# Cross-entropy with label smoothing: wider transfers in the first row, eleven shrinking ones in the second, buffers at multiples of 256 bytes, exponential sums in PSUM

## The chip, the cores and the metric

The kernel runs on one core of one Trainium2 chip. The metric is device time in microseconds of one execution; lower is better. The kernel before takes 84.87 us, the median of ten runs (84.70 to 84.98).

A core has several engines that run side by side, each through its own list of instructions: TensorE (matmul, PE in the profile), VectorE (DVE), ScalarE (ACT), GpSimd (POOL) and SyncE (SP), which here only issues DMA transfers. They wait for each other, and for transfers, on semaphores.

## The reference

The input is 256 rows of 32,000 logits in fp32, 256 labels and a smoothing of 0.1. For every row the loss is the negative sum of the smoothed targets times the log-probabilities:

```python
batch, num_classes = logits.shape                       # 256, 32000
log_probs = logits - np.max(logits, axis=-1, keepdims=True)
log_probs = log_probs - np.log(np.sum(np.exp(log_probs), axis=-1, keepdims=True))
smooth_targets = np.full((batch, num_classes), smoothing / num_classes)
for i, label in enumerate(labels):
    smooth_targets[i, label] = 1.0 - smoothing + smoothing / num_classes
return (-np.sum(smooth_targets * log_probs, axis=-1)).astype(np.float32)
```

The targets of a row sum to one, so the loss of a row is the logarithm of its sum of exponentials, minus `smoothing / num_classes` times the sum of its logits, minus `1 - smoothing` times the logit at its label. The kernel computes these three things. It does not subtract the maximum.

## The kernel before

The 256 rows are put on 128 partitions, two rows in each: partition p holds rows 2p and 2p + 1, one after the other, 64,000 columns in all. The kernel goes through the columns from left to right, first row first, in pieces whose widths stand in `WIDTHS` (lines 17 to 20): four of 8000 for the first row, and ten for the second, from 8000 down to 832.

For each piece there are three steps.

- `load` (line 156) issues one DMA transfer from SP's queue, 128 rows of one piece each. The very first piece goes in two halves, one from SP's queue and one from ScalarE's; a hook (`_issue_first_transfers_at_start`, line 40) moves these two issues to the start of the program. Pieces of 4736 columns or more rotate through three buffers of 8000 columns (`ring`); a piece that finds its buffer still in use makes SP wait until both VectorE and ScalarE are done with the old content, and all later issues stand behind it. Each smaller piece has a buffer of its own (`tail`).
- `sum_logits` (line 170) lets VectorE add the left half of the piece to the right half, with an accumulator that sums the result over the columns. The elementwise result goes to a scratch place (`jd`) and is not used.
- `sum_exps` (line 183) lets ScalarE compute the exponentials of the piece, again with an accumulator. The elementwise result, bf16, is not used either: for pieces over `TURN_MAX` = 3648 columns it goes to the one scratch place `ja`, for smaller ones to three places `jt` in turn.

An operation with an accumulator is two instructions in the profile: the main one, and a short READ_ACCUMULATOR that writes the 128 sums to their destination.

Around this, GpSimd loads the labels, gathers the logits at the labels and scales them (lines 104 to 152), and makes the identity matrix that TensorE needs for transposes.

The sums of the first row lie side by side in `sums0` (SBUF). When its four pieces are done, GpSimd adds them in two steps (`half`), ScalarE takes the logarithm (line 216), GpSimd puts the loss together (lines 218 to 224), TensorE turns the column of 128 losses into a row (`row_of`, line 190), and VectorE copies it to `res` (line 226).

The sums of the second row are finished in three layers, so that little is left after the last piece: the logit sums of the first eight pieces lie in `xsum` and the exponential sums of the first seven in `esum`, and are reduced to `done[0]` (lines 255 and 258) after VectorE's part of the third piece from the end. The last but two and the last but one exponential sums, and the last two logit sums, come through two small pairs (`pair0`, `pair1`), which are added to it (line 263). The exponential sum of the last piece goes to `elast` in PSUM and is the input of the last logarithm, with the sum of all the others as its bias (line 279). TensorE transposes both results, VectorE combines them to `res` (line 284), and SP stores the 256 losses.

Five pieces before the last, twenty matmul passes without use (`warm`, line 270) keep TensorE busy on the piece just loaded.

The order of the instructions on each engine is that of the program text, except where `tc.issue_after` names an instruction after which the next ones are to stand. The framework assigns the buffers and puts the semaphore waits in front of the instructions that need them.

Of the kernel before, what the change touches and what calls it, by code (L numbers as in the profile page):

```python
# [8 lines left out]
FP32 = mybir.dt.float32  # L9
BF16 = mybir.dt.bfloat16  # L10
I32 = mybir.dt.int32
ALU = mybir.AluOpType
AF = mybir.ActivationFunctionType
# [1 line left out]


WIDTHS = (
    (8000, 8000, 8000, 8000),
    (8000, 6272, 4736, 3648, 2688, 2048, 1536, 1216, 1024, 832),
)  # L20

RING_MIN = 4736

TURN_MAX = 3648

WARM_LEFT, WARM_COLS = 5, 256


def _exp_ln_table(arch: str) -> int | None:
# [30 lines left out]
def kernel(  # L60
# [7 lines left out]
    nc = tc.nc  # L68
    nc.at_finalize(_issue_first_transfers_at_start)
    B, C = logits.shape  # L70
    P = nc.NUM_PARTITIONS
    R = B // P
# [4 lines left out]
    c_small = eps / float(C)  # L77
    c_big = 1.0 - eps

    ring = ctx.enter_context(tc.tile_pool(name="ring", bufs=3))  # L80
    tail = ctx.enter_context(tc.tile_pool(name="tail", bufs=1))
    junk = ctx.enter_context(tc.tile_pool(name="junk", bufs=1))
    turn = ctx.enter_context(tc.tile_pool(name="turn", bufs=3))
    small = ctx.enter_context(tc.tile_pool(name="small", bufs=1))

    psum = ctx.enter_context(
        tc.tile_pool(name="psum", bufs=1, space=bass.MemoryType.PSUM)
    )

    tbl = _exp_ln_table(nc.m.arch)  # L90
    if tbl is not None:
        nc.scalar.add_instruction(  # L92
            mybir.InstLoadActFuncSet(
                name=nc.get_next_instruction_name(),
# [7 lines left out]
    x = logits.rearrange("(p r) c -> p (r c)", r=R)  # L102
# [3 lines left out]
        out=lab[:], in_=labels.bitcast(I32).rearrange("(p f) -> p f", p=P)  # L106
    )
    rowoff = small.tile([P, R], I32, name="rowoff", tag="rowoff")
    for r in range(R):
        nc.gpsimd.iota(  # L110
            out=rowoff[:, r : r + 1],
# [6 lines left out]
        out=flat_idx[:],  # L118
        in0=rowoff[:],
        in1=lab[:].rearrange("p (r two) -> p r two", two=2)[:, :, 0:1],  # L120
        op=ALU.add,
    )
    gat = small.tile([P, R], FP32, name="gat", tag="gat")
    for r in range(R):
        nc.gpsimd.indirect_dma_start(  # L125
            out=gat[:, r : r + 1],
            out_offset=None,
            in_=logits[:],
# [8 lines left out]

    label_weight = c_big / c_small
    xsum = small.tile([P, len(WIDTHS[-1]) + 1], FP32, name="xsum", tag="xsum")
    esum = small.tile([P, len(WIDTHS[-1])], FP32, name="esum", tag="esum")  # L140
    weighted = [
        small.tile([P, 1], FP32, name=f"weighted{r}", tag=f"weighted{r}")[:]
        for r in range(R - 1)
# [1 line left out]
    for r in range(R):  # L145
        nc.gpsimd.tensor_scalar(  # L146
            out=weighted[r],
            in0=gat[:, r : r + 1],
# [4 lines left out]

    res = small.tile([1, P, R], FP32, name="res", tag="res")

    def load(w: int, col: int, name: str):
        if w >= RING_MIN:
            xt = ring.tile([P, max(WIDTHS[0])], FP32, name="xt", tag="xt")
        else:
            xt = tail.tile([P, w], FP32, name=name, tag=name)  # L160
        if col == 0:

            h = w // 2
            nc.sync.dma_start(out=xt[:, :h], in_=x[:, :h])
            nc.scalar.dma_start(out=xt[:, h:w], in_=x[:, h:w])
        else:
            nc.sync.dma_start(out=xt[:, :w], in_=x[:, col : col + w])  # L167
        return xt

    def sum_logits(xt, w: int, out: bass.AP):  # L170
        h = w // 2
        jd = junk.tile([P, max(WIDTHS[0]) // 2], FP32, name="jd", tag="jd")
        return nc.vector.scalar_tensor_tensor(  # L173
            out=jd[:, :h],
            in0=xt[:, :h],
            scalar=1.0,
            in1=xt[:, h:w],
            op0=ALU.mult,
            op1=ALU.add,
            accum_out=out,  # L180
        )

    def sum_exps(xt, w: int, out: bass.AP) -> None:
        if w > TURN_MAX:
            ja = junk.tile([P, max(WIDTHS[0])], BF16, name="ja", tag="ja")
        else:
            ja = turn.tile([P, TURN_MAX], BF16, name="jt", tag="jt")
        nc.scalar.activation(out=ja[:, :w], in_=xt[:, :w], func=AF.Exp, accum_out=out)  # L188

    def row_of(column: bass.AP, name: str):  # L190

        row = psum.tile([1, P], FP32, name=name, tag=name)
        nc.tensor.transpose(out=row[:], in_=column, identity=ident[:])  # L193
        return row

    col = 0
    for r in range(R - 1):
        n = len(WIDTHS[r])
        sums = small.tile([P, 2, n], FP32, name=f"sums{r}", tag=f"sums{r}")
        for t, w in enumerate(WIDTHS[r]):  # L200
            xt = load(w, col, f"xl{r}_{t}")
            col += w
            sum_logits(xt, w, sums[:, 0, t : t + 1])
            sum_exps(xt, w, sums[:, 1, t : t + 1])


        while n > 1:
            assert n % 2 == 0
            n //= 2
            half = small.tile([P, 2, n], FP32, name=f"half{r}_{n}", tag=f"half{r}_{n}")  # L210
            nc.gpsimd.tensor_tensor(  # L211
                out=half[:], in0=sums[:, :, :n], in1=sums[:, :, n:], op=ALU.add
            )
            sums = half
        lse = small.tile([P, 1], FP32, name=f"lse{r}", tag=f"lse{r}")
        nc.scalar.activation(out=lse[:], in_=sums[:, 1, :], func=AF.Ln)  # L216
        lin = small.tile([P, 1], FP32, name=f"lin{r}", tag=f"lin{r}")
        nc.gpsimd.tensor_tensor(out=lin[:], in0=sums[:, 0, :], in1=weighted[r], op=ALU.add)
        scaled = small.tile([P, 1], FP32, name=f"scaled{r}", tag=f"scaled{r}")
        nc.gpsimd.tensor_scalar(  # L220
            out=scaled[:], in0=lin[:], scalar1=-c_small, scalar2=None, op0=ALU.mult
        )
        loss = small.tile([P, 1], FP32, name=f"loss{r}", tag=f"loss{r}")
        nc.gpsimd.tensor_tensor(out=loss[:], in0=scaled[:], in1=lse[:], op=ALU.add)  # L224
        loss_t = row_of(loss[:], f"loss_t{r}")
        nc.vector.tensor_copy(out=res[:, :, r : r + 1], in_=loss_t[:])  # L226

    r = R - 1  # L230
    n = len(WIDTHS[r])
    elast = psum.tile([P, 1], FP32, name="elast", tag="elast")
    pairs = [
        small.tile([P, 2], FP32, name=f"pair{i}", tag=f"pair{i}") for i in range(2)
    ]
    done = [
        small.tile([P, 2], FP32, name=f"done{i}", tag=f"done{i}") for i in range(3)
    ]
    warm = psum.tile([P, WARM_COLS], FP32, name="warm", tag="warm")
    for t, w in enumerate(WIDTHS[r]):  # L240
        left = n - 1 - t
        xt = load(w, col, f"xl{r}_{t}")
        col += w
        part = sum_logits(
            xt, w, xsum[:, t + 1 : t + 2] if left > 1 else pairs[1 - left][:, 0:1]
        )
        if left == 0:
            sum_exps(xt, w, elast[:])
        elif left <= 2:
            sum_exps(xt, w, pairs[2 - left][:, 1:2])  # L250
        else:
            sum_exps(xt, w, esum[:, t : t + 1])
        if left == 2:
            with tc.issue_after(part.ins):
                nc.vector.tensor_reduce(
                    out=done[0][:, 0:1], in_=xsum[:, : t + 2], axis=AX.X, op=ALU.add
                )
                nc.vector.tensor_reduce(
                    out=done[0][:, 1:2], in_=esum[:, :t], axis=AX.X, op=ALU.add
                )  # L260
        elif left < 2:
            i = 1 - left
            nc.vector.tensor_tensor(  # L263
                out=done[i + 1][:], in0=done[i][:], in1=pairs[i][:], op=ALU.add
            )
        if left == WARM_LEFT:


            for i in range(w // WARM_COLS):
                nc.tensor.matmul(  # L270
                    warm[:],
                    lhsT=ident[:],
                    rhs=xt[:, i * WARM_COLS : (i + 1) * WARM_COLS],
                    start=True,
                    stop=True,
                )

    lse = small.tile([P, 1], FP32, name=f"lse{r}", tag=f"lse{r}")
# [6 lines left out]
        out=res[:, :, r : r + 1],  # L285
        in0=lin_row[:],
        scalar=-c_small,
        in1=lse_t[:],
# [4 lines left out]
        out=out.rearrange("(g i) -> g i", g=1), in_=res[:].rearrange("g p r -> g (p r)")  # L293
# [36 lines left out]
```

## Time and profile before

| | us |
|---|---|
| median of ten runs | 84.87 |
| the profiled execution, in all | 84.89 |
| its span, from the first to the last instruction of the profile | 83.1 |
| ScalarE busy | 58.8 |
| VectorE busy | 37.1 |
| TensorE matmul busy | 7.3 |
| GpSimd busy | 5.9 |
| bytes moved by DMA | 32.77 MB, 394 GB/s over the span |
| start of the last exponential (832 columns) | 79.18 |
| start of the last logarithm | 80.15 |
| start of the last VectorE instruction (`res`) | 80.77 |

The profile is of one execution. Its own time is 84.89, 1.8 more than its span; the difference lies before the first and after the last instruction that the profile shows. All times below are counted from the start of the span.

The chain of waits, followed back from the end, goes through DMA for 64% of the span and through ScalarE for 32%. ScalarE sits idle for 19.9 us before its exponentials of pieces in the ring, and VectorE for 33.5 us before its sums of them, each time until a transfer lands. From 67.66 on, ScalarE works without a break that the chain shows: the seven exponentials of the smaller pieces, then the logarithm.

Of the instruction shapes that matter here, one exponential of 8000 columns takes 6.870 us, of 6272 columns 5.430, of 832 columns 0.879; one VectorE sum of 8000 columns 4.325, of 832 columns 0.592; an accumulator read on ScalarE 0.186 into SBUF and 0.149 into PSUM, on VectorE 0.082.

### The profile page before, as it was taken

Reading aid. Unit: us, or ns where it says so; the run is one execution under the profiler, and the core shown is the slowest. Engines: PE = TensorE matmul, PEld = TensorE weight load, DVE = VectorE, ACT = ScalarE, POOL = GpSimd, SP = SyncE. Lnnn points to the kernel's source line nnn. Section 1 sums busy time; section 2 is a strip of 40 time slices with the busy share of each in tenths; the row PEclk is TensorE's granted clock in tenths of the full one; section 3 lists DMA queues with packets and bytes.
Section 4 is the critical chain, followed back from the end, with each engine's and each line's share of the span. In section 5 each row is a group of like instructions: output and inputs, shape, how many; then the busy total and the mean of one; then the engine's idle time right before and its main releaser. Section 6 shows DMA issues by size and latency. Waiting matters only on the chain.

```text
span 83.1 us, 230 instructions
## 1 busy us (share of the span) xinstructions
PE 7.3 (9%) x23; PEld 5.3 (6%) x23; DVE 37.1 (45%) x35; ACT 58.8 (71%) x31; POOL 5.9 (7%) x19
## 2 busy tenths in 40 slices
PE   0000000000000000000000010000000000899220
PEld 0000000000000000000000000000000000778000
DVE  0000005950595009910397018922944735754860
ACT  5000005997599809994399908997999999999960
POOL 3201630041000000000000040000000000000000
PEclk9999999999999999999999999999999999999996
DMA  5999999998999899979997998998999999999600
GB/s 123 408 448 408 454 424 447 493 401 354 478 493 416 354 462 493 431 339 462 493 431 339 462 440 386 447 495 343 438 417 428 435 411 410 416 410 411 274 0 0
DMA packets 2258, 32.77 MB, mean 394 GB/s; under 512 B 337, under 2 KB 338, under 8 KB 850
## 3 DMA queue, kind: packets, MB, share of 16 engines
q1 hardware_dynamic: 2018, 30.72, 87.4%
q10 hardware_dynamic: 144, 2.05, 5.8%
q0 software_dynamic: 96, 0.00, 0.1%
HBM read 32.77 MB, written 0.00 MB: 394 GB/s over the span
## 4 chain that ended last, share of the span: by engine, by line
DMA 64%; ACT 32%; issue 1%; SPq 0%; PE 0%; DVE 0%; ACTq 0%
DMA xt<-in_logits_dram 40%; DMA xl<-in_logits_dram 23%; ACT ja L188 17%; ACT jt L188 15%; SPq L167 0%; PE lse_t L193 0%; DVE res L284 0%; ACT lse L279 0%; ACTq L188 0%
## 5 line engine op out<-in xcount | busy, mean ns | idle before, releaser
L188 ACT ACTIVATE ja<-xt 128x8000 bf16<-128x8000 f32 (+2 forms) x7 | 43.9, 6276 | 20.0 <-DMA xt<-in_logits_dram 19.9
L173 DVE SCALAR_TENSOR_TENSOR jd<-xt 128x4000 f32<-128x4000 f32 (+2 forms) x7 | 27.7, 3954 | 33.5 <-DMA xt<-in_logits_dram 33.5
L188 ACT ACTIVATE jt<-xl 128x3648 bf16<-128x3648 f32 (+6 forms) x7 | 12.2, 1748 | 0.1
L173 DVE SCALAR_TENSOR_TENSOR jd<-xl 128x1824 f32<-128x1824 f32 (+6 forms) x7 | 7.9, 1125 | 5.2 <-DMA xl<-in_logits_dram 5.0
L270 PE MATMUL warm<-xl,ident 128*128 128x256 f32 x20 | 6.4, 493 | 21.4 <-DMA xl<-in_logits_dram 21.4
L270 PEld LDWEIGHTS warm<-xl,ident 128*128 128x128 f32 x20 | 5.0, 257 | 22.6 <-DMA xl<-in_logits_dram 21.7
L193 PE MATMUL loss_t<-ident,loss 128*1 128x128 f32 x1 | 0.4, 373 | 49.2 <-POOL loss L224 49.2
L193 PEld LDWEIGHTS loss_t<-ident,loss 128*1 128x1 f32 x1 | 0.1, 79 | 49.2 <-POOL loss L224 49.2
L226 DVE COPY res<-loss_t 1x128 f32<-1x128 f32 x1 | 0.3, 280 | 4.5 <-PE loss_t L193 4.5
L211 POOL TENSOR_TENSOR half<-sums 128x4 f32<-128x4 f32 x1 | 0.2, 198 | 28.3 <-ACT ja L188 28.3
L125 POOL DMA_INDIRECT gat<-in_logits_dram,flat_idx x2 | 2.0, 1001 | 0.7 <-POOL ident masks.py:199 0.4
L92 ACT ACT_TABLE_LOAD x1 | 1.3, 1283 | 0.9 <-PEq L311 0.9
L146 POOL TENSOR_SCALAR weighted<-gat 128x1 f32<-128x1 f32 x1 | 0.9, 927 | 5.6 <-DMA gat<-in_logits_dram,flat_idx 5.6
L188 ACT ACTIVATION_READ_ACCUMULATOR ja<-xt 128x1 f32 x7 | 1.3, 186 | 0.0
L188 ACT ACTIVATION_READ_ACCUMULATOR jt<-xl 128x1 f32 x7 | 1.3, 181 | 0.0
L105 POOL DMA_DIRECT2D lab<-in_labels_dram x1 | 0.8, 768 | 1.0 <-POOLq L311 1.0
L216 ACT ACTIVATE lse<-half 128x1 f32<-128x1 f32 x1 | 0.2, 203 | 0.6 <-POOL half L211 0.6
L173 DVE DVE_READ_ACCUMULATOR jd<-xt 128x1 f32 x7 | 0.6, 82 | 0.0
L117 POOL TENSOR_TENSOR flat_idx<-rowoff,lab 128x2 int32<-128x2 int32 x1 | 0.2, 195 | 5.4 <-DMA lab<-in_labels_dram 5.4
L173 DVE DVE_READ_ACCUMULATOR jd<-xl 128x1 f32 x7 | 0.6, 82 | 0.0
L193 PE MATMUL lin_t<-ident,done 128*1 128x128 f32 x1 | 0.3, 270 | 2.7 <-DVE done L263 2.7
L282 DVE COPY lin_row<-lin_t 1x128 f32<-1x128 f32 x1 | 0.3, 279 | 0.4 <-PE lin_t L193 0.4
(20 smaller groups left out, 3.8 us busy)
## 6 DMA issues: line engine op xcount, KB each, us to landing
xt<-in_logits_dram SPq DMA_DIRECT2D x4, 4000.0 KB, 21.1
xt<-in_logits_dram SPq DMA_DIRECT2D x1, 3136.0 KB, 19.4
xt<-in_logits_dram SPq DMA_DIRECT2D x1, 2368.0 KB
xt<-in_logits_dram SPq DMA_DIRECT2D x1, 2000.0 KB, 11.5
xt<-in_logits_dram ACTq DMA_DIRECT2D x1, 2000.0 KB, 13.1
xl<-in_logits_dram SPq DMA_DIRECT2D x1, 1824.0 KB, 19.5
xl<-in_logits_dram SPq DMA_DIRECT2D x1, 1344.0 KB, 22.3
xl<-in_logits_dram SPq DMA_DIRECT2D x1, 1024.0 KB, 24.3
```

The source lines that it names most:

```text
L92: nc.scalar.add_instruction(mybir.InstLoadActFuncSet(name=nc.get_next_instruction_name(), act_func_set_id=tbl, ins=[], outs=[],))
L105: nc.gpsimd.dma_start(out=lab[:], in_=labels.bitcast(I32).rearrange("(p f) -> p f", p=P))
L117: nc.gpsimd.tensor_tensor(out=flat_idx[:], in0=rowoff[:], in1=lab[:].rearrange("p (r two) -> p r two", two=2)[:, :, 0:1], op=ALU.add,)
L125: nc.gpsimd.indirect_dma_start(out=gat[:, r : r + 1], out_offset=None, in_=logits[:], in_offset=bass.IndirectOffsetOnAxis(ap=flat_idx[:, r ...
L146: nc.gpsimd.tensor_scalar(out=weighted[r], in0=gat[:, r : r + 1], scalar1=label_weight, scalar2=None, op0=ALU.mult,)
L173: return nc.vector.scalar_tensor_tensor(out=jd[:, :h], in0=xt[:, :h], scalar=1.0, in1=xt[:, h:w], op0=ALU.mult, op1=ALU.add, accum_out=out,)
L188: nc.scalar.activation(out=ja[:, :w], in_=xt[:, :w], func=AF.Exp, accum_out=out)
L193: nc.tensor.transpose(out=row[:], in_=column, identity=ident[:])
L211: nc.gpsimd.tensor_tensor(out=half[:], in0=sums[:, :, :n], in1=sums[:, :, n:], op=ALU.add)
L226: nc.vector.tensor_copy(out=res[:, :, r : r + 1], in_=loss_t[:])
L270: nc.tensor.matmul(warm[:], lhsT=ident[:], rhs=xt[:, i * WARM_COLS : (i + 1) * WARM_COLS], start=True, stop=True,)
L282: nc.vector.tensor_copy(out=lin_row[:], in_=lin_t[:])
```

## The change

The first row is loaded in three pieces instead of four (8000, 12480 and 11520 columns) and the second in eleven instead of ten, from 8640 down to 576 columns.

There is no ring any more. Three wide buffers hold the three pieces of the first row. `FOLLOW = (1, 2, 6)` says how many pieces of the second row follow in each of them, side by side: 8640 in the first, 6400 and 4608 in the second, and the six from 3392 to 832 in the third. The last two pieces have buffers of their own. A place of 384 bytes per partition (`pad`) is put ahead of the buffers. In the kernel before, the first buffer starts at byte 16,512 of each partition, which is 128 over a multiple of 256, and all others at the same distance from one; in the changed kernel all of them start at multiples of 256, from 16,896 on. The first piece is cut at 3968 columns instead of 4000, so that both halves start at such multiples, in the memory and in the buffer.

There are two scratch places `jt` instead of three, for pieces of up to 4608 columns, and `ja` and `jd` are wider.

The exponential sums of the second row (`esum`, eight columns, and both pairs) lie in PSUM instead of SBUF. The work that finishes the first row moves into a function that is called after the first piece of the second row; in it, the logarithm stands on ScalarE behind the exponential of that piece, and the copy on VectorE behind its sum. GpSimd adds the three partial sums one after the other. The warming matmuls run six pieces before the last, on 2496 columns: eighteen passes instead of twenty.

```diff
 WIDTHS = (
-    (8000, 8000, 8000, 8000),
-    (8000, 6272, 4736, 3648, 2688, 2048, 1536, 1216, 1024, 832),
+    (8000, 12480, 11520),
+    (8640, 6400, 4608, 3392, 2496, 1856, 1408, 1088, 832, 704, 576),
 )
-RING_MIN = 4736
-TURN_MAX = 3648
-WARM_LEFT, WARM_COLS = 5, 256
+FOLLOW = (1, 2, 6)
+TURN_MAX = 4608
+PAD = 384
+WARM_LEFT, WARM_COLS = 6, 256
...
-    ring = ctx.enter_context(tc.tile_pool(name="ring", bufs=3))
+    pad = ctx.enter_context(tc.tile_pool(name="pad", bufs=1))
+    pad.tile([nc.NUM_PARTITIONS, PAD // 4], FP32, name="pad", tag="pad")
+    wide = ctx.enter_context(tc.tile_pool(name="wide", bufs=1))
...
-    turn = ctx.enter_context(tc.tile_pool(name="turn", bufs=3))
+    turn = ctx.enter_context(tc.tile_pool(name="turn", bufs=2))
...
-    esum = small.tile([P, len(WIDTHS[-1])], FP32, name="esum", tag="esum")
+    esum = psum.tile([P, len(WIDTHS[-1]) - 3], FP32, name="esum", tag="esum")
...
-    def load(w: int, col: int, name: str):
-        if w >= RING_MIN:
-            xt = ring.tile([P, max(WIDTHS[0])], FP32, name="xt", tag="xt")
-        else:
-            xt = tail.tile([P, w], FP32, name=name, tag=name)
+    buffers = []
+    for r in range(R):
+        for b in range(len(FOLLOW)):
+            t = sum(FOLLOW[:b])
+            parts = (WIDTHS[0][b : b + 1], WIDTHS[1][t : t + FOLLOW[b]])
+            widths = parts[r]
+            w = max(sum(parts[0]), sum(parts[1]))
+            buf = wide.tile([P, w], FP32, name=f"wide{b}_{r}", tag=f"wide{b}")
+            at = 0
+            for v in widths:
+                buffers.append(buf[:, at : at + v])
+                at += v
+    for t in range(sum(FOLLOW), len(WIDTHS[1])):
+        w = WIDTHS[1][t]
+        buffers.append(tail.tile([P, w], FP32, name=f"tail{t}", tag=f"tail{t}")[:])
+
+    def load(w: int, col: int):
+        xt = buffers.pop(0)
         if col == 0:
-            h = w // 2
+            h = w // 128 * 64
             nc.sync.dma_start(out=xt[:, :h], in_=x[:, :h])
             nc.scalar.dma_start(out=xt[:, h:w], in_=x[:, h:w])
         else:
-            nc.sync.dma_start(out=xt[:, :w], in_=x[:, col : col + w])
+            nc.sync.dma_start(out=xt, in_=x[:, col : col + w])
         return xt
...
+    def finish_first_row(part, exps) -> None:
+        total = sums[:, :, 0:1]
+        for t in range(1, n):
+            acc = small.tile([P, 2, 1], FP32, name=f"acc{t}", tag=f"acc{t}")
             nc.gpsimd.tensor_tensor(
-                out=half[:], in0=sums[:, :, :n], in1=sums[:, :, n:], op=ALU.add
+                out=acc[:], in0=total, in1=sums[:, :, t : t + 1], op=ALU.add
             )
+            total = acc[:]
...
-        lse = small.tile([P, 1], FP32, name=f"lse{r}", tag=f"lse{r}")
-        nc.scalar.activation(out=lse[:], in_=sums[:, 1, :], func=AF.Ln)
+        lse = small.tile([P, 1], FP32, name="lse0", tag="lse0")
+        with tc.issue_after(exps.ins):
+            nc.scalar.activation(out=lse[:], in_=total[:, 1, :], func=AF.Ln)
...
-        nc.vector.tensor_copy(out=res[:, :, r : r + 1], in_=loss_t[:])
+        with tc.issue_after(part.ins):
+            nc.vector.tensor_copy(out=res[:, :, 0:1], in_=loss_t[:])
...
     pairs = [
-        small.tile([P, 2], FP32, name=f"pair{i}", tag=f"pair{i}") for i in range(2)
+        psum.tile([P, 2], FP32, name=f"pair{i}", tag=f"pair{i}") for i in range(2)
     ]
...
+        if t == 0:
+            finish_first_row(part, exps)
```

The order of the instructions on the engines is otherwise the same. The waits differ in one respect that the diff doesn't show. In the built program of the kernel before, an exponential of the smaller pieces waits for its load and, from the fourth on, for the exponential three before it, whose scratch place it takes. In the changed one, the exponentials of 4608, 3392, 2496, 1856, 1408 and 1088 columns each wait for their load and for the exponential just before them, whose sum goes to the same PSUM tile; those of 832, 704 and 576 columns do not. On VectorE, the sum of the 704-column piece waits for the exponentials of the 832-column piece, and that of the 576-column piece for the exponentials of the 704-column piece, because they share a pair in PSUM.

## The prediction

> **What bounds the kernel now.** I read the page first, its busy line and its slices, to see whether any engine is full; then the chain; then the instructions in order of time on VectorE and ScalarE, because the busy shares mix a stage that waits for loads with one that doesn't.
>
> From the page (busy time and share of the span; in the slices each figure is one fortieth of the span):
>
> ```profile
> span 83.1 us, 230 instructions
> PE 7.3 (9%) x23; PEld 5.3 (6%) x23; DVE 37.1 (45%) x35; ACT 58.8 (71%) x31; POOL 5.9 (7%) x19
> DMA  5999999998999899979997998998999999999600
> GB/s 123 408 448 408 454 424 447 493 401 354 478 493 416 354 462 493 431 339 462 493 431 339 462 440 386 447 495 343 438 417 428 435 411 410 416 410 411 274 0 0
> ```
>
> No compute engine is full, but the DMA line is from the second slice to the thirty-seventh. VectorE's starts in order of time give the arrivals, since it idles for each (start, duration, what; the bracket is the idle time before and what ended it):
>
> ```profile
> 50.27 4.33 DVE L173 SCALAR_TENSOR_TENSOR jd<-xt 128x4000 f32<-128x4000 f32 x1 [0.40 <-DMA xt<-in_logits_dram]
> 57.72 3.42 DVE L173 SCALAR_TENSOR_TENSOR jd<-xt 128x3136 f32<-128x3136 f32 x1 [3.12 <-DMA xt<-in_logits_dram]
> 63.36 2.62 DVE L173 SCALAR_TENSOR_TENSOR jd<-xt 128x2368 f32<-128x2368 f32 x1 [2.21 <-DMA xt<-in_logits_dram]
> ```
>
> Arrivals of 8000 columns are 9.49 apart (31.29, 40.78, 50.27), that of 1536 comes 1.88 after the one before it. So a transfer of w columns takes 1.1765 ns × w + 0.075 us: 512 bytes per column by 1.1765 ns is 435 GB/s. Loads bound the kernel up to the last arrival, near 79.1. ScalarE in the last stage:
>
> ```profile
> 70.81 0.19 ACT L188 ACTIVATION_READ_ACCUMULATOR jt<-xl 128x1 f32 x1
> 70.90 2.44 ACT L188 ACTIVATE jt<-xl 128x2688 bf16<-128x2688 f32 x1
> ...
> 78.12 1.06 ACT L188 ACTIVATE jt<-xl 128x1024 bf16<-128x1024 f32 x1
> 79.09 0.19 ACT L188 ACTIVATION_READ_ACCUMULATOR jt<-xl 128x1 f32 x1
> 79.18 0.88 ACT L188 ACTIVATE jt<-xl 128x832 bf16<-128x832 f32 x1
> 79.97 0.15 ACT L188 ACTIVATION_READ_ACCUMULATOR jt<-xl 128x1 f32 x1
> 80.15 0.26 ACT L279 ACTIVATE lse<-elast,done 128x1 f32<-128x1 f32 x1
> ```
>
> Three things are to be seen. An exponential starts while the accumulator read before it still runs (70.90 against 70.81 + 0.19), and 79.18 is exactly 78.12 + 1.06: without a wait the next starts when the last one's own row ends. The logarithm, which waits for the accumulator read, starts at 80.15, 0.03 after 79.97 + 0.15. And that one read, into PSUM, took 0.149, the others 0.186. The end on VectorE:
>
> ```profile
> 79.59 0.08 DVE L173 DVE_READ_ACCUMULATOR jd<-xl 128x1 f32 x1
> 79.78 0.16 DVE L263 TENSOR_TENSOR done<-done,pair 128x2 f32<-128x2 f32 x1
> 80.30 0.28 DVE L282 COPY lin_row<-lin_t 1x128 f32<-1x128 f32 x1 [0.36 <-PE lin_t L193]
> 80.77 0.28 DVE L284 SCALAR_TENSOR_TENSOR res<-lin_row,lse_t 1x128 f32<-1x128 f32 x1 [0.19 <-PE lse_t L193]
> ```
>
> The last sum is done at 79.94, 0.2 ahead of the logarithm, so VectorE is just off the path. What follows 80.77 (res, store, closing) is 2.3 us and stays. The profiled execution took 84.89: 1.8 lies outside the span. The median of the runs is 84.87, so span differences carry over as they are.
>
> **What the skill says.** The Trainium skill, "ScalarE: Activation LUTs", section "What ACT_TABLE_LOAD costs": an ACTIVATE with immediate operands is 186 ns + 0.833 N, neighbours overlap by about 93 ns. The trace has 6.870 for 8000 and 5.430 for 6272 columns, 0.8333 ns a column plus 0.203; and 0.879 for 832, where the sum goes to PSUM, 0.017 under that line. "Perfetto Trace Analysis", section "Optimizing Scalar/DVE Operations": the access overhead is about 93 ns for ScalarE on SBUF and 51 on PSUM, for VectorE 60 and 125, and the write-acknowledge half of a row overlaps the next instruction. The 37 ns between the two kinds of accumulator read agree; since it is the overlapped half that shrinks, PSUM gives nothing to an instruction that doesn't wait for it. "DMA: Bandwidth & Descriptors", sections "Where 436 GB/s comes from" and "How a descriptor splits into AXI transactions": 435.2 GB/s is the ceiling, which the slope above meets; a descriptor that starts off a 256-byte boundary fetches bytes it doesn't use. No row of this trace separates aligned from unaligned loads.
>
> **The change part by part.**
> *Widths.* There are fourteen SP transfers and one of ScalarE's queue on both sides, and the same bytes, so at equal cost each the last arrival doesn't move. From 21.81 (16,000 columns in), 4480 more columns give 27.08 for the 12480 chunk; then 40.71 (11520), 50.95 (8640), 58.55 (6400), 64.04, 68.11, 71.12, 73.37, 75.10, 76.46, 77.51, 78.41 and 79.16 (576). ScalarE finishes 12480 at 37.8, before 40.71, and 11520 at 50.6, before 50.95: idle until there, as now. The issue of 8640 needs the first chunk done (20.9 at the latest), those of 6400 and 4608, side by side in one buffer, the 12480 chunk (37.8, while 11520 and 8640 still keep the queue full to 50.95), the six in the third buffer, with the last two in order behind them, 11520 (50.6, queue full to 64.04). Each SP issue takes 0.33 to 0.43, eight in a row 3.4: hidden by the queue; without that cover each late issue would cost its delay. The first chunk may land up to 0.65 later, if one packet of 49,920 bytes instead of 32,000 gets between its own (17,920 bytes at a sixteenth of 435 GB/s); ScalarE's 6 us of idle time before 27.08 hide that, and later gathers have until 51.
> *Alignment.* The first buffer starts at byte 16,512 before, 128 over a multiple of 256, and at 16,896 after. At worst it gives nothing, at best all 0.075 a transfer. I take half, 0.038 (8 rows a DMA engine, four 32-byte beats of 1.18 ns each, an estimate with the DMA page's beats). Of that only the transfers ahead of ScalarE's last idle moment count, about 0.12 by 6400.
> *The first row's logarithm* moves behind the exponential of 8640: that one starts at 50.84 and runs 7.4, the logarithm's 0.20 fits before the arrival of 6400 (58.40): 0.02. Its five GpSimd sums (0.2 each), the transpose and the copy lie under 6400; nothing waits for them before the store.
> *ScalarE from 6400 on.* Start 58.42. Ten exponentials of 23,360 columns: 19.47, plus ten times 0.186 (the PSUM form) 1.86: 79.75 for the end of the last. It would be 79.92 with 0.203. Before: 80.06.
> *The new waits.* In the built program each exponential of 4608, 3392, 2496, 1856, 1408 and 1088 columns waits for its predecessor's accumulator, for they write one PSUM tile; before, in SBUF, a second-stage exponential waited only for the scratch of three earlier. The row of the PSUM read ends 0.057 after the ACTIVATE's row, and the waiter starts 0.032 later, as the logarithm shows: 0.089 each, six times 0.53. Behind them stand all later exponentials. The end: 80.28. The two scratch places cost nothing: their waits are for the second last exponential, 1 us back.
> *VectorE's new waits.* The sum of the 704 chunk now waits for ScalarE's 832, that of 576 for its 704, since they share the PSUM pairs. ScalarE ends 832 at 78.84 (accumulator 78.90), so: start 78.94, 0.525, PSUM read 0.075 (0.01 today plus 65 ns of the trace-analysis page's difference), hand-over 0.045, add 0.16: 79.75. Then 576: 79.77 + 0.458 + 0.075 + 0.045 + 0.16 = 80.51, against 79.94 today. The logarithm can start 0.09 later, 80.60, instead of at 80.37 by ScalarE alone; the copy chain from 80.51 (0.05, transpose 0.27, 0.04, copy 0.28, 0.11) reaches res at 81.26. Today 80.77. The bound for the PSUM reads is 0 to 0.13 each round.
> Sum: +0.49, made of -0.31 (ScalarE's work), +0.53 (waits) and +0.27 (VectorE). 84.87 + 0.49 = 85.36; I say 85.38, the longer forms weighing a little.
>
> **Rivals.**
> 1. *The waits are free:* PSUM acknowledges so early that the semaphore is there when the engine is ready anyway. Place: the six handovers. For it: the PSUM read is shorter. Against: the logarithm's 0.03 after it. Then ScalarE ends at 79.75, VectorE's chain at 79.95, res at 80.70: 84.80; with PSUM free for VectorE too 84.55. With VectorE's chain as priced, it decides only below 0.01 a handover. 10 in 100.
> 2. *Neither alignment nor the PSUM form gives anything:* +0.12 and +0.17 on the main sum, 85.65. For it: the DMA ceiling is already met in the slope, and the 0.017 is one row. 20 in 100.
> 3. *TensorE is cold at the transposes.* The warming matmuls take 18 passes instead of 20, from 71.1 to about 77.0, and the transposes come 0.7 later. "TensorE: Matmul & The Clock Gate", Part 1: an idle window of about 3.4 us halves the clock. The cold transpose of the first row took 0.37, the others 0.27: +0.2, 85.57. For it: the idle gap grows from 2.7 to 3.6. 10 in 100.
> 4. *Rows over 32 KB load more slowly.* 24,000 columns, 28 us; 2% is 0.6: 86.0. Nothing in the trace shows such a row. 5 in 100.
> The main course has 55.
>
> **How the numbers follow.** Main: 85.2 to 85.6. Rivals 2 and 3 reach 85.7; half of rival 1 and the tail above are left out: 85.0 to 85.8. A change of 0.2%, about what measurement can tell from none, is 84.70 to 85.04. Faster: half of rival 1, 6 in 100 with unknowns. Within: the rest of it and the main course's edge, 10. Slower: 84.
>
> **What would show it.** Right: ScalarE without idle for loads from 64 on, each of the six exponentials 0.07 to 0.11 behind its predecessor's row; VectorE's last two sums starting after ScalarE's accumulators rather than at an arrival; the logarithm near 80.6. Wrong: arrivals over 0.3 earlier (alignment under-priced), gaps under 0.02 (rival 1), arrivals of 12480 and 11520 over 0.3 late (rival 4), transposes of 0.37 (rival 3).

## The result and the profile after

| | us, median | against the kernel before |
|---|---|---|
| before | 84.88 (84.70 to 85.01, 28 runs) | |
| changed | 85.23 (85.11 to 85.34, 8 runs) | 1.0042, 95% interval 1.0033 to 1.0051 |

The changed kernel is slower by 0.35 us. The profiled execution took 85.22 and its span is 83.4, so again 1.8 lies outside the span.

The page of the changed kernel, busy time and slices as before:

```profile
span 83.4 us, 228 instructions
...
PE 6.7 (8%) x21; PEld 4.6 (6%) x21; DVE 37.0 (44%) x35; ACT 58.4 (70%) x31; POOL 10.2 (12%) x19
...
DMA  6999999999888899889996999999999999999300
```

The loads end earlier (the third last slice shows 3 where it showed 6) and the span is longer: more time passes after the last load. The chain of waits says the same, by engine, in shares of the span:

```profile
DMA 52%; ACT 40%; issue 4%; DVE 1%; PE 1%; ACTq 0%
```

DMA had 64% and ScalarE 32%. ScalarE in order of time, from the row where it stops waiting for loads (start, duration, what):

```profile
58.22 5.54 ACT L209 ACTIVATE ja<-wide 128x6400 bf16<-128x6400 f32 x1
...
71.10 2.28 ACT L209 ACTIVATE jt<-wide 128x2496 bf16<-128x2496 f32 x1
73.30 0.15 ACT L209 ACTIVATION_READ_ACCUMULATOR jt<-wide 128x1 f32 x1
73.48 1.75 ACT L209 ACTIVATE jt<-wide 128x1856 bf16<-128x1856 f32 x1
...
78.69 0.79 ACT L209 ACTIVATE jt<-tail 128x704 bf16<-128x704 f32 x1
79.38 0.17 ACT L209 ACTIVATION_READ_ACCUMULATOR jt<-tail 128x1 f32 x1
79.43 0.69 ACT L209 ACTIVATE jt<-tail 128x576 bf16<-128x576 f32 x1
80.00 0.18 ACT L209 ACTIVATION_READ_ACCUMULATOR jt<-tail 128x1 f32 x1
80.39 0.26 ACT L310 ACTIVATE lse<-elast,done 128x1 f32<-128x1 f32 x1 [0.21 <-DVE done L294]
```

Two kinds of handover are to be seen. The row of 2496 columns ends at 71.10 + 2.28 = 73.38; the next exponential, which waits for it, starts at 73.48, after the accumulator read (73.30 + 0.15) is done. All six waiting exponentials have such a gap, 0.091 to 0.093 each in the trace's own nanoseconds. The row of 704 columns ends at 79.48, and the next exponential, which does not wait, starts at 79.43: 0.05 *before* its predecessor's row ends. And the logarithm stands idle for 0.21 until VectorE's last sum is there:

```profile
78.84 0.53 DVE L194 SCALAR_TENSOR_TENSOR jd<-tail 128x352 f32<-128x352 f32 x1 [0.60 <-ACT jt L209]
79.29 0.14 DVE L194 DVE_READ_ACCUMULATOR jd<-tail 128x1 f32 x1
...
80.14 0.16 DVE L294 TENSOR_TENSOR done<-done,pair 128x2 f32<-128x2 f32 x1
...
81.12 0.28 DVE L315 SCALAR_TENSOR_TENSOR res<-lin_row,lse_t 1x128 f32<-1x128 f32 x1
```

VectorE's sum of the 704 piece starts at 78.84 because of ScalarE (the bracket), though the piece has been in its buffer since 77.75. Its accumulator read takes 0.14 where it took 0.08. TensorE's two transposes are slower too:

```profile
80.35 0.35 PE L216 MATMUL lin_t<-ident,done 128*1 128x128 f32 x1 [4.14 <-DVE done L294]
80.70 0.37 PE L216 MATMUL lse_t<-ident,lse 128*1 128x128 f32 x1
```

They took 0.27 each before. So `res` starts at 81.12 instead of 80.77, 0.35 later, which is the whole difference of the medians: 0.24 of it in the start of the logarithm (80.39 against 80.15), 0.11 behind it.

### The profile page after: what moved, and what is told of

The parts are those of the page before. It is cut to its first block, busy times and chain, and to the rows that moved or that the text cites. A ratio compares the mean times of both kernels' runs of the same rounds, so it can differ in the third digit from the quotient of the medians.

```text
span 83.4 us, 228 instructions
## 1 busy us (share of the span) xinstructions
PE 6.7 (8%) x21; PEld 4.6 (6%) x21; DVE 37.0 (44%) x35; ACT 58.4 (70%) x31; POOL 10.2 (12%) x19
## 4 chain that ended last, share of the span: by engine, by line
DMA 52%; ACT 40%; issue 4%; DVE 1%; PE 1%; ACTq 0%
DMA wide<-in_logits_dram 52%; ACT ja L209 24%; ACT jt L209 16%; DVE jd L194 1%; PE lse_t L216 0%; PE lin_t L216 0%; DVE res L315 0%; DVE done L294 0%; ACT lse L250 0%; ACTq L209 0%
## 5 line engine op out<-in xcount | busy, mean ns | idle before, releaser
L209 ACT ACTIVATE ja<-wide 128x8000 bf16<-128x8000 f32 (+4 forms) x5 | 40.2, 8043 | 20.9 <-DMA wide<-in_logits_dram 20.9
L194 DVE SCALAR_TENSOR_TENSOR jd<-wide 128x4000 f32<-128x4000 f32 (+11 forms) x12 | 34.6, 2879 | 39.0 <-DMA wide<-in_logits_dram 39.0
L209 ACT ACTIVATE jt<-wide 128x4608 bf16<-128x4608 f32 (+6 forms) x7 | 14.4, 2069 | 0.2
L301 PE MATMUL warm<-wide,ident 128*128 128x256 f32 x18 | 5.6, 480 | 11.7 <-DMA wide<-in_logits_dram 11.7
L301 PEld LDWEIGHTS warm<-wide,ident 128*128 128x128 f32 x18 | 4.4, 252 | 12.7 <-DMA wide<-in_logits_dram 12.0
L241 POOL TENSOR_TENSOR lin<-acc,weighted 128x1 f32<-128x1 f32 x1 | 4.6, 4602 | 0.1
L209 ACT ACTIVATE jt<-tail 128x704 bf16<-128x704 f32 (+1 forms) x2 | 1.4, 740 | 0.0
L194 DVE SCALAR_TENSOR_TENSOR jd<-tail 128x352 f32<-128x352 f32 (+1 forms) x2 | 1.0, 492 | 0.6 <-ACT jt L209 0.6
L209 ACT ACTIVATION_READ_ACCUMULATOR jt<-wide 128x1 f32 x7 | 1.1, 154 | 0.0
L194 DVE DVE_READ_ACCUMULATOR jd<-wide 128x1 f32 x12 | 1.0, 82 | 0.0
```

What stands on the lines that cost most here:

```text
L194: return nc.vector.scalar_tensor_tensor(out=jd[:, :h], in0=xt[:, :h], scalar=1.0, in1=xt[:, h:w], op0=ALU.mult, op1=ALU.add, accum_out=out,)
L209: return nc.scalar.activation(out=ja[:, :w], in_=xt[:, :w], func=AF.Exp, accum_out=out)
L241: nc.gpsimd.tensor_tensor(out=lin[:], in0=total[:, 0, :], in1=weighted[0], op=ALU.add)
L301: nc.tensor.matmul(warm[:], lhsT=ident[:], rhs=xt[:, i * WARM_COLS : (i + 1) * WARM_COLS], start=True, stop=True,)
```

## The experiments

The theory: the change consists of three parts that add up. Aligned buffers make the loads faster; the new widths alone change little; and the sums in PSUM cost more than alignment gains, through the waits. The rivals: the new widths are what costs; PSUM is slow in itself, with or without waits; or the waits cost nothing and the time is lost elsewhere. In every case the time of the kernel before is that of the runs beside it.

### Sums back in SBUF

```diff
-    esum = psum.tile([P, len(WIDTHS[-1]) - 3], FP32, name="esum", tag="esum")
+    esum = small.tile([P, len(WIDTHS[-1]) - 3], FP32, name="esum", tag="esum")
...
-        psum.tile([P, 2], FP32, name=f"pair{i}", tag=f"pair{i}") for i in range(2)
+        small.tile([P, 2], FP32, name=f"pair{i}", tag=f"pair{i}") for i in range(2)
```

> The changed kernel with the exponential sums of the second row and both pairs in SBUF again; widths and aligned buffers stay. Theory (the six PSUM handovers and VectorE's two waits are the loss): no exponential waits for its predecessor any more, the ten from 6400 on follow each other at 0.203 us + 0.833 ns a column, 58.22 + 21.50 gives 79.7 for the end of the last one and the logarithm at 79.8 instead of 80.39: 84.6 us (84.5 to 84.7), 0.6 under the changed kernel and under the kernel before. Rival (the widths, not PSUM, are the loss): within 0.1 of the changed kernel's 85.23.

Measured: 84.44 (6 runs) against 84.81; ratio 0.9947 (0.9934 to 0.9961). ScalarE, in order of time:

```profile
71.09 2.27 ACT L209 ACTIVATE jt<-wide 128x2496 bf16<-128x2496 f32 x1
73.26 0.19 ACT L209 ACTIVATION_READ_ACCUMULATOR jt<-wide 128x1 f32 x1
73.35 1.74 ACT L209 ACTIVATE jt<-wide 128x1856 bf16<-128x1856 f32 x1
...
79.94 0.26 ACT L310 ACTIVATE lse<-elast,done 128x1 f32<-128x1 f32 x1
```

71.09 + 2.27 is 73.36: no gap. Counted from the start of the 6400 columns (58.51 here, 58.22 in the changed kernel), the last exponential ends after 21.35 instead of 21.90, the logarithm starts after 21.43 instead of 22.17, `res` after 22.05 instead of 22.90. PSUM costs 0.55 on ScalarE, 0.19 more by VectorE's late sums, and 0.11 is lost behind the logarithm: 0.85, beside 0.81 from the two ratios (1.0042 - 0.9947, times 84.8). The 0.55 is six gaps (0.55) and longer rows (0.14: the ten rows are 21.50 in the changed kernel, 21.36 here), less the early starts (0.15). The widths are not what costs.

### Buffers off their multiples, with PSUM and without

```diff
-PAD = 384
+PAD = 256
```

> The changed kernel with the place ahead of the buffers 128 bytes smaller, so that every load buffer starts 128 bytes over a multiple of 256, as before. Theory (alignment brought the loads forward): arrivals from 8640 on 0.2 to 0.6 later than in the changed kernel, that of 6400 near 58.4 instead of 58.14, and since ScalarE is the limit from there, 85.5 us. Rival (wider transfers brought them forward): arrivals and time as in the changed kernel, 85.23.

Measured: 85.42 (6 runs), ratio 1.0071 (1.0057 to 1.0086). The 6400 columns landed at 58.42 instead of 58.14.

The same pad together with the sums in SBUF leaves of the change only the widths, the order of the buffers, the two scratch places, the warming on another piece and the first row's late finish:

> The changed kernel misaligned and with the sums in SBUF: what is left is the widths, the buffers that follow each other and the two scratch places. Theory (these are neutral): ScalarE starts 6400 at 58.5, 21.5 of work, last exponential ends at 80.05 as in the kernel before: 84.9 us. Rival (the eleven smaller pieces cost something of their own): 85.1 or more.

Measured: 84.77 (14 runs), ratio 0.9992 (0.9981 to 1.0003): no difference that the runs can tell (-0.16 to +0.03 us).

The trace's records of landings give the price of alignment. From the landing of the 12480 piece to that of the last one there are twelve transfers; they take 51.67 in the changed kernel (26.784 to 78.456) and 51.73 with sums in SBUF, but 52.08 in both kernels with the smaller pad: 0.41 and 0.35, or about 0.03 a transfer on the mean. (All eight aligned profiles with these widths lie between 51.66 and 51.78.)

### The kernel before with aligned buffers

```diff
+    pad = ctx.enter_context(tc.tile_pool(name="pad", bufs=1))
+    pad.tile([nc.NUM_PARTITIONS, 96], FP32, name="pad", tag="pad")
...
-            h = w // 2
+            h = w // 128 * 64
```

> The kernel before with a place of 384 bytes ahead of its buffers and the first piece cut at 3968, so that all its loads start at multiples of 256 bytes; nothing else. Theory: each of its transfers saves 0.04 us, the last arrival comes 0.5 earlier, ScalarE becomes the limit from the 2688 piece on and its last exponential ends near 79.6 instead of 80.06: 84.4 us. Rival (alignment does nothing here): 84.9.

Measured: 84.36 (6 runs), ratio 0.9942 (0.9927 to 0.9957). VectorE's sums of the 6272 and 4736 columns, which start when their loads land:

```profile
57.46 3.43 DVE L175 SCALAR_TENSOR_TENSOR jd<-xt 128x3136 f32<-128x3136 f32 x1 [3.08 <-DMA xt<-in_logits_dram]
...
63.03 2.63 DVE L175 SCALAR_TENSOR_TENSOR jd<-xt 128x2368 f32<-128x2368 f32 x1 [2.13 <-DMA xt<-in_logits_dram]
```

They started at 57.72 and 63.36 in the kernel before. From the landing of the first 16,000 columns to the last: 56.93 instead of 57.34, twelve transfers, 0.034 each on the mean. Nothing else of the change is needed for a kernel that is half a microsecond faster than the one before.

### The kernel before with its sums in PSUM

```diff
-    esum = small.tile([P, len(WIDTHS[-1])], FP32, name="esum", tag="esum")
+    esum = psum.tile([P, len(WIDTHS[-1])], FP32, name="esum", tag="esum")
...
-        small.tile([P, 2], FP32, name=f"pair{i}", tag=f"pair{i}") for i in range(2)
+        psum.tile([P, 2], FP32, name=f"pair{i}", tag=f"pair{i}") for i in range(2)
```

> The kernel before with its exponential sums and pairs in PSUM, nothing else. Theory: there ScalarE idles for the loads up to the 3648 piece, so of the waits only those of 2688, 2048 and 1536 fall on the path, 0.09 each, and the quicker starts of 1216, 1024 and 832 give back most; VectorE's two waits remain, 0.15 to 0.2 at the end: 84.95 us (84.85 to 85.1). Rival (PSUM costs the same wherever it is put, as in the changed widths): 85.4.

Measured: 85.04 (22 runs), ratio 1.0016 (1.0003 to 1.0029). The same waits cost 0.14 here, not 0.8:

```profile
73.39 0.15 ACT L188 ACTIVATION_READ_ACCUMULATOR jt<-xl 128x1 f32 x1
73.58 1.91 ACT L188 ACTIVATE jt<-xl 128x2048 bf16<-128x2048 f32 x1
...
79.18 0.90 ACT L188 ACTIVATE jt<-xl 128x832 bf16<-128x832 f32 x1
```

There are gaps of 0.09 ahead of 2688, 2048 and 1536 columns, and yet the last exponential starts at 79.18, exactly as in the kernel before. There the exponentials of 2048, 1536, 1216 and 1024 columns each start 0.02 to 0.08 after their piece has landed (78.12 after 78.04 for the last of them): on the old widths ScalarE still runs into the loads up to 78.12. That slack and the early starts ahead of 1216, 1024 and 832 columns (0.04, 0.05 and 0.06) pay for the gaps. What is left is VectorE: its last sums wait for ScalarE, and the logarithm starts at 80.27 instead of 80.15. So the price of the waits depends on the slack of the engine they stand on. On the changed widths ScalarE doesn't run into a load after 58.22, and every 0.09 is passed on to the end.

### Which PSUM tile costs: the pairs in SBUF

```diff
-        psum.tile([P, 2], FP32, name=f"pair{i}", tag=f"pair{i}") for i in range(2)
+        small.tile([P, 2], FP32, name=f"pair{i}", tag=f"pair{i}") for i in range(2)
```

> The changed kernel with only the two pairs back in SBUF; the other exponential sums stay in one PSUM tile. Theory: VectorE's last two sums no longer wait for ScalarE, the six handovers of 0.29 us + 0.833 ns a column stay, the logarithm starts when the last accumulator is read, near 80.32 instead of 80.39, and the two transposes no longer queue behind each other: 85.1 us, 0.1 to 0.2 under the changed kernel. Rival (VectorE's waits are most of the loss): 84.7 or less.

Measured: 85.14 (14 runs), ratio 1.0042 (1.0027 to 1.0057): the ratio of the changed kernel. The 0.1 to 0.2 expected from the pairs doesn't show in the times. The six gaps are there as in the changed kernel. By the traces, counted from the start of the 6400 columns, the pairs in PSUM hold the logarithm back by VectorE's late sums, 0.18, and give 0.06 of it back, since the last exponential ends after 21.90 instead of 21.96: 0.12 in all, which the two intervals can't tell from nothing. Against all sums in SBUF the logarithm is 0.62 late here (22.05 instead of 21.43): most of the loss lies in `esum`, with its six waits.

### The wait without PSUM

```diff
-    turn = ctx.enter_context(tc.tile_pool(name="turn", bufs=2))
+    turn = ctx.enter_context(tc.tile_pool(name="turn", bufs=1))
```

together with the sums in SBUF: each small exponential now waits for its predecessor because of the one scratch place.

> The changed kernel with its sums in SBUF and one scratch place instead of two: the eight exponentials from 3392 to 576 wait for their predecessor because of the scratch, not because of PSUM. Theory (it is the wait): each step is 0.093 + 0.032 longer than a row without a wait, 0.33 us + 0.833 ns a column, eight times 0.125 is 1.0 above the same kernel with two places: 85.4 us. Rival (waiting is free, PSUM was the cost): 84.4.

Measured: 85.65 (6 runs), ratio 1.0099 (1.0081 to 1.0117), 0.25 more than expected:

```profile
73.34 0.19 ACT L209 ACTIVATION_READ_ACCUMULATOR jt<-wide 128x1 f32 x1
73.56 1.75 ACT L209 ACTIVATE jt<-wide 128x1856 bf16<-128x1856 f32 x1
```

The gap is 0.124 here, and there are eight (from 3392 to 576 columns): 0.99. The row of an exponential that has waited is longer as well, by 0.017: the 1856 columns take 1.75 here and 1.74 where nothing waits. Eight times 0.124 + 0.017 is 1.13, by which the stretch on ScalarE grows against the kernel with sums in SBUF (22.48 instead of 21.35). The 0.13 in the rows had not been expected; the remaining 0.1 of the miss is not explained. So it is the wait that costs, whatever it is for. The gap is shorter with PSUM (0.09), as the accumulator read is (0.15 instead of 0.19).

### PSUM without the wait

Two PSUM tiles take the eight sums in turn, so that each exponential waits only for the last but one; the pairs are in SBUF, and two more small reductions on VectorE put the two tiles together.

```diff
-    esum = psum.tile([P, len(WIDTHS[-1]) - 3], FP32, name="esum", tag="esum")
+    esums = [psum.tile([P, 4], FP32, name=f"esum{i}", tag=f"esum{i}") for i in range(2)]
+    ehalf = small.tile([P, 2], FP32, name="ehalf", tag="ehalf")
...
-            exps = sum_exps(xt, w, esum[:, t : t + 1])
+            exps = sum_exps(xt, w, esums[t % 2][:, t // 2 : t // 2 + 1])
```

> The changed kernel with the eight exponential sums in two PSUM tiles in turn, so that each exponential waits for the last but one, and the pairs in SBUF; VectorE gets two small reductions more. Theory (the wait is the cost, the place is a gain): ScalarE's step falls from 0.295 us + 0.833 ns a column to about 0.145, it keeps up with the loads again, the last exponential ends near 79.35 and the logarithm starts near 79.45: 84.2 us (84.0 to 84.4). Rival (the place costs, whatever is waited for): the steps stay near 0.29 and the time near that of the kernel with the pairs in SBUF, 85.1.

Measured: 84.63 (84.24 to 85.16, 11 runs), ratio 0.9972 (0.9950 to 0.9994). The time missed what was expected; the trace did not:

```profile
72.94 1.75 ACT L210 ACTIVATE jt<-wide 128x1856 bf16<-128x1856 f32 x1
74.59 0.15 ACT L210 ACTIVATION_READ_ACCUMULATOR jt<-wide 128x1 f32 x1
74.64 1.37 ACT L210 ACTIVATE jt<-wide 128x1408 bf16<-128x1408 f32 x1
```

72.94 + 1.75 is 74.69; the next starts at 74.64. The logarithm starts 21.27 after the start of the 6400 columns, against 21.43 with sums in SBUF, though it waits 0.06 for VectorE and its two more reductions, and the span is 82.5 (median of the 11 runs), against 82.65. But these executions take 2.05 more than their spans, on the mean (1.74 to 2.19), while all the others take 1.79 to 1.82.

### What lies outside the span

The kernel with sums in SBUF, given the same three reductions, tells whether it is PSUM or the two instructions:

```diff
+                for i in range(2):
+                    nc.vector.tensor_reduce(
+                        out=ehalf[:, i : i + 1], in_=esum[:, 4 * i : 4 * i + 4], axis=AX.X, op=ALU.add
+                    )
                 nc.vector.tensor_reduce(
-                    out=done[0][:, 1:2], in_=esum[:, :t], axis=AX.X, op=ALU.add
+                    out=done[0][:, 1:2], in_=ehalf[:], axis=AX.X, op=ALU.add
                 )
```

> The changed kernel with all sums in SBUF, and with the three small reductions of the two-tile kernel instead of two (four sums, four sums, and their two results): the same list of instructions as the two-tile kernel, without sums in PSUM. That kernel's execution took 2.05 us more than its span, on the mean of 11 runs; all other kernels so far 1.79 to 1.82. Theory A, what is added outside the span comes with the two more instructions: the time less the span is about 2.05 here too, and the time 84.7. Theory B, it belongs to the two PSUM tiles or to that set of runs: the time less the span is 1.8, and the time is that of the SBUF kernel, 84.45.

> The two-tile kernel once more, beside the others of this call. If the 2.05 between its time and its span belongs to its program: again 2.05, span 82.5, time 84.6. If it belonged to that set of runs: 1.8, and 84.3.

> The kernel before, aligned, once more, so that it stands beside the two-tile kernel in the same call: 84.36 again, span 82.55. By time the two-tile kernel is then behind it by 0.25 or level with it; by span level.

Measured, against 84.87 for the kernel before: 84.73 with three reductions in SBUF (10 runs, ratio 0.9981, 0.9969 to 0.9993), 84.62 for two PSUM tiles again (22 runs, 0.9974, 0.9960 to 0.9989), 84.38 for the aligned kernel before (6 runs, 0.9940, 0.9926 to 0.9954). The time less the span is 2.03, 2.00 and 1.79. It comes with the two instructions, not with PSUM.

A last kernel has one reduction less: the sum of the first tile goes to a fifth place of the second tile.

```diff
-                for i in range(2):
-                    nc.vector.tensor_reduce(
-                        out=ehalf[:, i : i + 1], in_=esums[i][:], axis=AX.X, op=ALU.add
-                    )
                 nc.vector.tensor_reduce(
-                    out=done[0][:, 1:2], in_=ehalf[:], axis=AX.X, op=ALU.add
+                    out=esums[1][:, 4:5], in_=esums[0][:], axis=AX.X, op=ALU.add
+                )
+                nc.vector.tensor_reduce(
+                    out=done[0][:, 1:2], in_=esums[1][:], axis=AX.X, op=ALU.add
                 )
```

> The two-tile kernel with one small reduction less: the sum of the first tile is written to a fifth place of the second tile, and one reduction over five follows. One more instruction than the changed kernel, two being what came with 0.23 us outside the span. Expected by the steps of the two-tile kernel: span 82.5. If the time outside the span grows evenly with instructions, it is 1.91 and the time 84.4; if it is a step that one instruction stays below, 1.80 and 84.3, which is level with or a little ahead of the kernel before aligned (84.36, 84.38); if the first instruction already takes the step, 2.03 and 84.55.

Measured: 84.35 (84.25 to 84.47, 6 runs) against 84.86, ratio 0.9942 (0.9928 to 0.9955); span 82.45, time less span 1.92. With 35, 36 and 37 VectorE instructions in the profile, 1.80, 1.92 and 2.03 lie outside on the mean: 0.12 for each. With 37 single executions scatter from 1.73 to 2.19, with 36 from 1.88 to 1.97. What happens there the profile doesn't show; it stays open, as does whether instructions of another kind or engine cost the same. The kernel is as fast as the kernel before with aligned buffers, and both beat the two kernels of this study by 0.5 to 0.9.

Put together, as time against the kernel before (ratio less one, times 84.8):

| | misaligned | aligned |
|---|---|---|
| old widths, SBUF | 0 | -0.49 |
| old widths, PSUM | +0.14 | not tried |
| new widths, SBUF | -0.07 | -0.45 |
| new widths, PSUM | +0.60 | +0.36 |

Alignment is worth 0.49 on the old widths, where ScalarE runs into the loads almost to the end and all transfers count, and 0.38 and 0.24, each uncertain by some 0.15, on the new ones, where only those up to 6400 columns do.

## Why the prediction was right

The forecast was slower, 85.38, in 85.0 to 85.8; it is slower, 85.23, by the mechanism named: six waits on ScalarE and VectorE's late sums. That the number comes within 0.15 is in part luck, since errors of opposite sign met: a gain of 0.17 that did not come beside one of 0.15 that was denied, and alignment priced 0.12 too low beside 0.07 more than forecast between the logarithm and `res`. Point by point:

- **Widths: no effect.** Right within the noise; shown by the kernel that has the widths without alignment and PSUM (0.9992, 0.9981 to 1.0003).
- **Arrivals.** 12480 columns were expected to be in at 27.08 and landed at 26.78; from there to the start of the 6400 columns 31.34 was expected and 31.44 measured. So what came too early lies in the first 27 us. The 6400 columns landed 0.26 ahead of the forecast 58.40; over 0.3 had been named as the sign that alignment was priced too low. The first piece landed 0.56 later than before (13.80 instead of 13.24); up to 0.65 had been allowed for, and ScalarE's idle time hid it, as said.
- **Alignment.** Half of the 0.075 per transfer, 0.038, was a choice between two bounds; on the mean it is 0.03 to 0.04. But the 0.12 up to the start of the 6400 columns was too small; by the times it is 0.24. The first 32,000 columns are in at 40.58 to 40.69 in the four misaligned profiles, whatever their widths, and at 40.28 to 40.39 in six of the eight aligned ones with wide pieces (40.60 and 40.64 in the other two). That is mostly 0.3, where four transfers at 0.034 make 0.14. (With the old widths aligned they are in at 40.46 and 40.49.) Why the start gains more, and not in every execution, is open.
- **Exponentials in their PSUM form, 0.186 instead of 0.203.** This step was wrong. The ten rows add up to 21.50, which is 0.203 each and 0.8333 ns a column. The shorter row in the kernel before was not PSUM's: it belonged to the one exponential there that had nothing to wait for. With the sums in SBUF and no waits, the nine rows from 4608 to 576 columns take 0.186 to 0.189 and 0.8333 ns a column; with one scratch place, where those from 3392 on wait, 0.203 again. What PSUM does give was missed. "PSUM gives nothing to an instruction that doesn't wait for it" is the reverse of what the trace shows: an exponential that doesn't wait starts 0.04 to 0.06 before the row of its predecessor ends, 0.15 for the three of them. The figures of the Trainium skill cited there ("Perfetto Trace Analysis", section "Optimizing Scalar/DVE Operations": 93 ns on SBUF, 51 on PSUM) are of the engine's own busy time, and their difference, 42 ns, is about this; it was the reading that was wrong. The two errors, +0.17 and -0.15, cancel by luck.
- **Six handovers of 0.089.** Right: 0.091 to 0.093, 0.55 in all instead of 0.53. The last exponential ended at 80.12 instead of 80.28, mostly by the start 0.20 earlier: 58.22 + 21.50 + 0.55 - 0.15 is 80.12.
- **VectorE behind ScalarE.** Right in kind: the sum of 704 columns starts 0.03 after ScalarE's accumulator read, its own read from PSUM costs 0.06 more (0.065 was expected), and VectorE, not ScalarE, releases the logarithm, 0.18 after ScalarE by itself would have done (its read ends at 80.18, and 0.03). 0.23 was expected. The logarithm came at 80.39 rather than 80.60, again mostly by the earlier start.
- **Rival 3, a cold TensorE,** came true in this execution: transposes of 0.35 and 0.37, after an idle gap of 4.14 (before 2.68), and `lse_t` queued behind `lin_t`. `res` came 0.11 later after the logarithm than before. The misaligned kernel, with the same instructions and transposes of 0.27, has 0.03 of that from the queueing alone, so 0.08 belongs to the slow transposes of this execution. The profiles of the other kernels don't make a rule of it: 0.27 after gaps of 3.44, 3.23 and 2.90, but 0.37 after 2.23 in the kernel with only the pairs in SBUF, and in the one with three reductions in SBUF 0.27 for the first and 0.37 for the second, 0.42 later. The ends of the warming matmuls are modelled, so the gaps are not sharp.
- **Rival 1, free waits,** fell with the gaps of 0.09; **rival 4, slow long rows,** with the landings: in the two misaligned kernels with pieces of 12480 and 11520 columns the first 32,000 are in at 40.58 and 40.66, in the kernel before, with pieces of 8000, at 40.69. Of **rival 2** one half, the PSUM form, was true, but in the place of the gain came the early starts.

## What to carry to other kernels

Before small results are moved from one memory to another, look at which tile they share there: eight accumulators in one tile made a chain of waits of 0.09 us each, and two tiles in turn took it away. A wait costs what the engine's slack doesn't cover, so the same edit was worth 0.14 with widths that leave ScalarE idle now and then, and 0.7 to 0.8 with widths that don't. Where a change has a gain and a loss in it, try the gain alone: 384 bytes of padding, with the first piece cut to match, were the best part here.

## What the runs showed of the hardware that was not expected

- Exponentials with accumulators in PSUM follow each other 0.14 to 0.16 us plus 0.833 ns a column apart where none waits (0.17 for one in each trace of the two-tile kernels), in SBUF 0.19 to 0.20; with a wait 0.295 in PSUM and 0.33 in SBUF. In SBUF the row itself is 0.017 longer when the exponential had to wait, for a load or for another instruction (0.203 instead of 0.186).
- A destination in SBUF that starts 128 bytes off a multiple of 256 costs 0.03 to 0.04 us in a transfer of 128 rows, on the mean of twelve. Single transfers differ, and not in the order of their widths: between the means of the aligned and the misaligned kernels with the new widths it is 0.05 for 8640 and for 1408 columns, nothing for 6400 and for 576. The addresses in memory were the same with the larger and the smaller pad, so it is the destination. "DMA: Bandwidth & Descriptors", section "How a descriptor splits into AXI transactions", of the Trainium skill has this for the side that is read; these runs show it for the side that is written.
- A GpSimd addition of 128 values took 4.60 instead of 0.19. GpSimd in the kernel before, where VectorE was idle, and then both engines in the changed one:

```profile
48.36 0.19 POOL L218 TENSOR_TENSOR lin<-half,weighted 128x1 f32<-128x1 f32 x1
```

```profile
50.63 4.66 DVE L194 SCALAR_TENSOR_TENSOR jd<-wide 128x4320 f32<-128x4320 f32 x1 [4.02 <-DMA wide<-in_logits_dram]
50.74 4.60 POOL L241 TENSOR_TENSOR lin<-acc,weighted 128x1 f32<-128x1 f32 x1
```

  VectorE's sum of 4320 + 4320 columns runs from 50.63 to 55.29, and the addition ends 0.05 after it. The Trainium skill, "SBUF — State Buffer", section "Who interferes with whom", says that a VectorE instruction with two inputs in SBUF and a GpSimd instruction that reads SBUF exclude each other, the later one blocking until the first is done; the trace agrees. Here it was hidden: the loss of the first row also needs the logarithm, which came at 57.99, more than 2 us after GpSimd had caught up.
- Each VectorE instruction added to the last stage, of the two that were tried, lengthened the execution by 0.12 us on the mean outside the span of the profile, beside what it did inside. Of two kernels with nearly equal spans one can be slower by 0.2 for this alone, so spans are compared only after the time less the span has been looked at.
